# Gate logits and the branch merge of a hybrid attention/recurrence layer with tokens as rows

## The chip, the core and the metric

One Trainium2 chip, one of its NeuronCores. The number is the device time of one execution in microseconds, the median of several runs.

## What is computed

One layer of a backbone over 256 latent tokens with a prefix of 256 context tokens, width 2048, everything in 32-bit floating point. The mixer part matters here, cut to its core:

```python
p = h @ w_in                       # h: normed, modulated tokens
c_q, c_kv, k_r, hg_q, hg_ff, hg_fb, hg_i, hg_g, gate_logits = split(p)
attn_o = attention(...)            # 8 heads of 128, latent and context keys
hg_o = rmsnorm(hgrn2(...)) * silu(hg_g)          # 8 heads of 128
y_a = attn_o.reshape(256, 1024) @ w_br_mla       # (256, 2048)
y_h = hg_o.reshape(256, 1024) @ w_br_hgrn        # (256, 2048)
g = sigmoid(gate_logits)                         # (256, 2, 2048)
out = (g[:, 0] * y_a + g[:, 1] * y_h) @ w_out
x = x + gt_a * rmsnorm(out)        # then a SwiGLU part, 2048 -> 2 x 5632 -> 2048
```

## The kernel before, in words

A matmul takes a stationary operand (128 x up to 128) and a moving one (128 x up to 512). Each 32-bit operand is split into a high part H, rounded to the format that TensorE multiplies quickly, and a low rest L; a product is then three: high by high, high by low, low by high. Activations are split once. Weights come in tiles of 1 MB (`load_w`, L100, on SP's queue, three buffers `raw`), and each tile is split in two halves of 1024 columns: ACT casts H (L108), DVE subtracts to get L (L110). There are three buffers of each, so ACT casts a half when TensorE has read the half that was in the buffer.

Two layouts of a product occur. With channels as rows the weight is stationary (128 x 128) and the tokens move: `mm3` (L144) and, for the latent tokens alone, `mm_wide`, where one product has H against both token parts (512 columns, L148) and one L against the high part (256 columns, L149). With tokens as rows 128 tokens are stationary and 512 weight columns move: `project_tok` (L825), which serves the output projection and the SwiGLU part, with two accumulators `pst`, one for each half of the tokens.

PSUM has eight banks of 128 x 512. Four belong to the pool `pj` (the long accumulators), which rotates through them, four to `px` (short ones).

The stages in order: adaLN vectors and the first projections; eight recurrent heads (`hgrn_head`); attention in four pairs of heads. Since attention is made of short steps, 32 blocks of the gate logits (`gates`, each 16 pairs of L148 and L149) are put between them. A pair of heads begins with `att_q`: queries `pq` and rope queries `pr` from one weight tile (L654, L144), then values `pv2` from another (L670), then a gate block; then come keys (`att_k`), scores with softmax (`att_s`, whose rope half uses 64 of 128 rows, L698), transposes (`att_t`) and values (`att_v`). Gate logits go to DRAM (`sgd`) by POOL's queue, since no room is left for them, and come back in the merge. The merge runs over 16 blocks of 128 channels: both branches as 48 products of 256 columns in one bank (`psb`, L760), sigmoid on ACT, product on DVE (L763), sum of the branches on POOL (L765), split into `units`. Jobs that multiply a tile of adaLN weights on DVE (`mod_job`) are strewn over all stages. After the output projection comes the SwiGLU part; its product rows are turned by TensorE transposes (`turn`, L961).

The order on each engine is not the one in the text: a scheduler places instructions by estimated times of its own, and each engine then works strictly in its order.

## Time and profile before

| | us |
|---|---|
| median of three runs | 1741.63 (1738.98, 1741.84, 1741.63) |
| the profiled execution, time | 1740.55 |
| the profiled execution, span from first to last instruction | 1738.8 |
| gates and attention, from the first gate product to the first merge product | 533.1 to 808.4 |
| merge, to the first product of the output projection | 808.4 to 900.7 |
| TensorE (PE) busy | 1694.0 |
| VectorE (DVE), ScalarE (ACT), GpSimd (POOL) busy | 1089.0, 766.2, 51.7 |
| mean granted clock of TensorE | 0.991 |

PE's weight loads (PEld) are listed apart from its products. A product's duration in the profile runs from its start to a modelled end, and the next one starts before that; the distance between starts tells what a product costs. "Idle before <- releaser" names what ended a wait.

### The profile page before, as it was taken

How to read it: one execution, taken by the hardware profiler on the slowest of the kernel's cores; microseconds unless marked ns; L12 is line 12 of the kernel's file. 1: busy time of each engine (PE TensorE's matmuls, PEld its weight loads, DVE VectorE, ACT ScalarE, POOL GpSimd, SP SyncE). 2: the span in 40 equal slices, each digit the busy share in tenths (PEclk: the TensorE clock that was granted, in tenths of full speed). 3: DMA queues.
4: the chain of work that ended last, by engine and by line, in shares of the span. 5: the costliest groups of instructions: out<-in, count | busy, mean ns of one | idle time of the engine just before them, and what ended most of it. 6: DMA issues, size and time to landing. Idle time of an engine off the chain costs nothing.

```text
span 1738.8 us, 22134 instructions
## 1 busy us (share of the span) xinstructions
PE 1694.0 (97%) x8715; PEld 1410.4 (81%) x8715; DVE 1089.0 (63%) x1619; ACT 766.2 (44%) x1086; POOL 51.7 (3%) x81
## 2 busy tenths in 40 slices
PE   6898999999999999999999899999999999999997
PEld 4457888888888888889998788888888888888886
DVE  5335777777778766666765765664456655544456
ACT  5225443343345444445544554444444443344443
POOL 0100000000000000001210000000000000000000
PEclk9899999999999999999999999999999999999999
DMA  9983455655556565578766456665566665555653
GB/s 389 357 330 148 162 178 194 217 194 194 180 183 231 193 253 189 194 290 303 278 222 224 167 218 242 234 234 187 194 242 233 234 233 208 194 193 185 214 193 121
DMA packets 60247, 383.78 MB, mean 221 GB/s; under 512 B 7104, under 2 KB 7920, under 8 KB 16880
## 3 DMA queue, kind: packets, MB, share of 16 engines
q1 hardware_dynamic: 55328, 368.15, 58.1%
q0 software_dynamic: 4096, 13.11, 1.9%
q8 instruction: 68, 1.11, 0.3%
q10 hardware_dynamic: 720, 1.12, 0.2%
q14 instruction: 35, 0.29, 0.0%
HBM read 376.03 MB, written 6.32 MB: 220 GB/s over the span
## 4 chain that ended last, share of the span: by engine, by line
PE 94%; DMA 2%; DVE 2%; ACT 1%; issue 0%; SPq 0%; DVEq 0%; ACTq 0%
PE pst L825 45%; PE ps L144 13%; PE ps L148 11%; PE ps L149 5%; PE psb L760 5%; PE pre L144 3%; DMA raw<-in_wm_dram 2%; PE pm L282 1%; PE pst L919 1%; PE psS L698 1%; PE po L722 1%; PE psS L695 1%; PE pv L670 1%; PE pq L654 1%; PE pk L144 1%; PE pgt L961 1%
## 5 line engine op out<-in xcount | busy, mean ns | idle before, releaser
L110 DVE TENSOR_TENSOR wL<-raw,wH 128x1024 fp32r<-128x1024 f32 x480 | 589.8, 1231 | 480.0 <-ACT wH L108 458.2
L108 ACT CAST wH<-raw 128x1024 fp32r<-128x1024 f32 x480 | 503.4, 1050 | 710.8 <-PE pst L825 393.1
L825 PE MATMUL pst<-wH,hx 128*128 128x512 f32 x2272 | 660.6, 390 | 0.0
L825 PEld LDWEIGHTS pst<-wH,hx 128*128 128x128 f32 x2272 | 425.6, 188 | 87.7
L825 PE MATMUL pst<-wL,hx 128*128 128x512 f32 x1136 | 402.2, 389 | 0.0
L148 PE MATMUL ps<-hx,wH 128*128 128x512 f32 x832 | 300.6, 402 | 2.8 <-DVE lat L367 2.8
L825 PEld LDWEIGHTS pst<-wL,hx 128*128 128x128 f32 x1136 | 213.2, 188 | 44.4
L149 PE MATMUL ps<-hx,wL 128*128 128x256 f32 x832 | 235.6, 284 | 0.0
L144 PE MATMUL ps<-hx,wH 128*128 128x512 f32 x672 | 212.5, 395 | 0.0
L148 PEld LDWEIGHTS ps<-hx,wH 128*128 128x128 f32 x832 | 156.9, 189 | 40.2 <-DVE lat L367 3.1
L346 DVE CUSTOM_DVE_ANT_0 raw<-raw,cb 128x2048 f32<-128x2048 f32 x64 | 146.1, 2283 | 31.8 <-DMA raw<-in_wm_dram 31.6
L149 PEld LDWEIGHTS ps<-hx,wL 128*128 128x128 f32 x832 | 157.7, 190 | 3.3 <-DVE mx L700 1.1
L144 PEld LDWEIGHTS ps<-hx,wH 128*128 128x128 f32 x672 | 125.0, 188 | 25.2
L144 PE MATMUL ps<-hx,wL 128*128 128x512 f32 x336 | 131.7, 392 | 0.0
L144 PEld LDWEIGHTS ps<-hx,wL 128*128 128x128 f32 x336 | 63.1, 188 | 12.8
L144 PE MATMUL pre<-hx,wH 128*128 128x512 f32 (+1 forms) x204 | 66.7, 410 | 5.4 <-ACT hx L201 5.3
L144 PEld LDWEIGHTS pre<-hx,wH 128*128 128x128 f32 x204 | 39.6, 204 | 25.6 <-ACT hx L201 10.8
L760 PE MATMUL psb<-hx,wH 128*128 128x256 f32 x256 | 46.8, 283 | 0.0
L760 PE MATMUL psb<-hC,wH 128*128 128x256 f32 x256 | 46.8, 283 | 0.0
L760 PEld LDWEIGHTS psb<-hx,wH 128*128 128x128 f32 x256 | 39.9, 192 | 0.0
L760 PEld LDWEIGHTS psb<-hC,wH 128*128 128x128 f32 x256 | 39.9, 192 | 0.0
L282 PE MATMUL pm<-raw,cst 128*32 128x512 f32 (+1 forms) x320 | 34.9, 538 | 4.3 <-DMA raw<-in_wm_dram 4.2
(256 smaller groups left out, 1416.8 us busy)
## 6 DMA issues: line engine op xcount, KB each, us to landing
raw<-in_wm_dram SPq DMA_DIRECT2D x96, 1024.0 KB, 4.9
raw<-in_wfi_dram SPq DMA_DIRECT2D x88, 1024.0 KB, 4.8
raw<-in_win_dram SPq DMA_DIRECT2D x73, 1024.0 KB, 4.8
raw<-in_wfo_dram SPq DMA_DIRECT2D x44, 1024.0 KB, 4.8
raw<-in_wbr_dram SPq DMA_DIRECT2D x16, 1024.0 KB, 5.6
raw<-in_wout_dram SPq DMA_DIRECT2D x16, 1024.0 KB, 4.9
raw<-in_wqk_dram SPq DMA_DIRECT2D x4, 1024.0 KB, 5.3
sgd<-sgx POOLq DMA_DIRECT2D x16, 256.0 KB, 5.0
```

What stands on the lines that cost most here:

```text
L108: nc.scalar.copy(H, raw[:, o:o + n])
L110: nc.vector.tensor_tensor(L, raw[:, o:o + n], H.bitcast(F32), op=ALU.subtract)
L144: nc.tensor.matmul(o, l, r, start=(first and i == 0), stop=(last and i == len(seq) - 1))
L148: nc.tensor.matmul(ps, w[0], act.rearrange("p e t -> p (e t)"), start=first, stop=False)
L149: nc.tensor.matmul(ps[:, 0:T], w[1], act[:, 0, :], start=False, stop=last)
L282: nc.tensor.matmul(pm[32 * (k % 4):32 * (k % 4) + 32, 0:n], cst[:, k], raw[:, kk * n:(kk + 1) * n], start=(k < 4), stop=(k >= KD - 4))
L346: nc.vector.tensor_tensor_reduce(out=raw, in0=raw, in1=cbt[0], scale=1.0, scalar=0.0, op0=ALU.mult, op1=ALU.add, accum_out=mod2[:, i // KD ...
L654: nc.tensor.matmul(pq[:, i * T:(i + 1) * T], l, r, start=(k == 0 and i == 0 and z == 0), stop=(k == 3 and i == 1 and z == 2))
L670: nc.tensor.matmul(pv[:, i, :], ckvs[:, k, l, ts_], r, start=(i == 0 and k == 0 and z == 0), stop=(i == 1 and k == 1 and z == 2))
L695: nc.tensor.matmul(psS, qn[a][:, i * T + qb * P:i * T + (qb + 1) * P], kn[b], start=(n == 0), stop=False)
L760: nc.tensor.matmul(ps[:, br * T:(br + 1) * T], l, r, start=(br == 0 and k == 0 and z == 0), stop=(br == 1 and k == NH - 1 and z == 2))
L825: mm = nc.tensor.matmul(ps[hf], l, r, start=(k == 0 and n == 0), stop=(k == nk - 1 and n == 2))
```

## The change

The gate logits and both branches of the merge go from channels as rows to tokens as rows. `gates` now works on chunks of 512 of the 4096 gate columns: four calls share two accumulators `psg`, one for each token half, and each call takes one 1 MB tile with 4 of the 16 k blocks, 24 products of 512 columns. After the fourth call the two rows are copied out (one by ACT, one by DVE) and stored. The merge has four chunks of 512 channels; each branch of a chunk goes through `project_tok`; the gates are multiplied onto the accumulators, POOL adds the branches, and the rows are turned back into `units` by eight transposes a chunk (`turn_merged`), called after the first tile of the next chunk. The long banks are no longer one pool of four but two pairs, `pj` and `pk`: other users alternate, the gate accumulators take `pk`, the attention tiles `pj`. The adaLN jobs in the merge keep their number, five.

```diff
+    def bank(name, tag=None, shape=(P, 512)):
+        if tag is None:
+            tag = ("pj", "pk")[n_bank[0] % 2]
+            n_bank[0] += 1
+        return pj.tile(list(shape), F32, tag=tag, name=name)
...
     def gates(b):
-        j = b // 2
+        cc, q = b // 4, b % 4
         if b % 2 == 0:
             mod_job(1)
-        w = split_w(load_w(win[47 + b - NPRE]))
-        ps = pj.tile([P, 512], F32, tag="pj", name="ps")
-        for k in range(KD):
-            mm_wide(ps, w(k * P, P), hx[:, 0, k], k == 0, k == KD - 1)
-        half = sgx[:, j % 4, (b % 2) * T:(b % 2 + 1) * T]
-        nc.scalar.copy(half, ps[:, 0:T])
-        nc.vector.tensor_tensor(half, half, ps[:, T:2 * T], op=ALU.add)
-        if b % 2 == 1:
-            nc.gpsimd.dma_start(sgd[j], sgx[:, j % 4, :])
+        w = split_w(load_w(wg[cc, q]))
+        if q == 0:
+            gate_ps[:] = [bank("psg", "pk") for _ in range(2)]
+        for k in range(4 * q, 4 * q + 4):
+            H, L = w(k % 4 * 512, 512)
+            for hf in range(2):
+                aH, aL = (hx[:, 0, k, e, hf * P:(hf + 1) * P] for e in range(2))
+                for n, (l, r) in enumerate(((aH, H), (aL, H), (aH, L))):
+                    nc.tensor.matmul(gate_ps[hf], l, r, start=(k == 0 and n == 0), stop=(k == KD - 1 and n == 2))
+        if q == 3:
+            for hf in range(2):
+                row = sgx[:, (2 * cc + hf) % 4, :]
+                (nc.scalar.copy if hf else nc.vector.tensor_copy)(row, gate_ps[hf])
+                nc.gpsimd.dma_start(sgd[cc, hf], row)
         step()
...
     def att_q(p, A):
-        pq = pj.tile([P, 512], F32, tag="pj", name="pq")
-        pr = pj.tile([P, 512], F32, tag="pj", name="pr")
+        pq = bank("pq", "pj")
+        pr = bank("pr", "pj")
...
-            pv = pj.tile([P, 2, T], F32, tag="pj", name="pv2")
+            pv = bank("pv2", "pj", (P, 2, T))
...
-    for j in range(KD):
-        sg = sgx[:, (4 + j) % 8, :]
-        nc.gpsimd.dma_start(sg, sgd[j])
-        w = split_w(load_w(wbr[j]))
-        ps = pj.tile([P, 512], F32, tag="pj", name="psb")
-        for br, src in enumerate(([aT[:, h] for h in range(NH)], hgT)):
-            for k in range(NH):
-                H, L = w(br * 1024 + k * P, P)
-                for z, (l, r) in enumerate(((H, src[k][:, 0, :]), (H, src[k][:, 1, :]), (L, src[k][:, 0, :]))):
-                    nc.tensor.matmul(ps[:, br * T:(br + 1) * T], l, r, start=(br == 0 and k == 0 and z == 0),
-                                     stop=(br == 1 and k == NH - 1 and z == 2))
-        nc.scalar.activation(sg, sg, AF.Sigmoid)
-        nc.vector.tensor_tensor(sg, ps, sg, op=ALU.mult)
-        m = wk.tile([P, T], F32, tag="hf", name="m", bufs=2)
-        nc.gpsimd.tensor_tensor(m, sg[:, 0:T], sg[:, T:2 * T], op=ALU.add)
-        dst = units[j]
-        split_act(dst, m)
-        mg.append(dst)
-        if j % 3 == 0 and j < 13:
-            mod_job(1)
...
+    def turn_merged(c):
+        for b in range(0, 4, 2):
+            pt = px.tile([P, 2, T], F32, tag="px", name="pmt")
+            for i in range(2):
+                for hf in range(2):
+                    nc.tensor.matmul(pt[:, i, hf * P:(hf + 1) * P], m_row[c][hf][:, (b + i) * P:(b + i + 1) * P], ident,
+                                     is_transpose=True, start=(i + hf == 0), stop=(i + hf == 2))
+            for i in range(2):
+                dst = units[4 * c + b + i]
+                split_act(dst, pt[:, i])
+                mg.append(dst)
+
+    m_row = []
+    for c in range(4):
+        sg = []
+        for n in range(4):
+            sg.append(sgx[:, 4 * (c + 1) % 8 + n, :])
+            nc.gpsimd.dma_start(sg[n], sgd[2 * c + n // 2, n % 2])
+        for br, src in enumerate(([aT[:, h] for h in range(NH)], hgT)):
+            ps = project_tok(lambda q: wbr[br, c, q], NH, lambda k: src[k], True, True, None,
+                             (lambda: turn_merged(c - 1)) if c > 0 and br == 0 else None)
+            for hf in range(2):
+                g = sg[2 * br + hf]
+                nc.scalar.activation(g, g, AF.Sigmoid)
+                nc.vector.tensor_tensor(g, ps[hf], g, op=ALU.mult)
+                if br == 1:
+                    nc.gpsimd.tensor_tensor(sg[hf], sg[hf], g, op=ALU.add)
+        m_row.append(sg)
+        mod_job(2 if c == 0 else 1)
...
         ps = project_tok(lambda q: wout[c, q], KD, lambda k: mg[k], True, True,
-                         pairs([wide(u) for u in spare[:8]]) if c == 3 else None)
+                         pairs([wide(u) for u in spare[:8]]) if c == 3 else None,
+                         (lambda: turn_merged(3)) if c == 0 else None)
```

The weights are laid out anew to suit (`wg`, `wbr` as tiles of 4 k blocks by 512 columns). The scheduler makes another order of it. Three places follow; the numbers of the lines are those of the kernel that the order belongs to, and a number in a name tells two tiles of one name apart.

PE at the end of `att_q` of the second pair of heads, before: queries, rope queries, and the values right behind.

```order
L654 MATMUL pq<-cqkv,wH 128x256 x2
L654 MATMUL pq<-cqkv,wL 128x256
L144 MATMUL pr<-cqkv,wH 128x256 x2
L144 MATMUL pr<-cqkv,wL 128x256
L670 MATMUL pv_5200<-wH,cqkv 128x256 x2
L670 MATMUL pv_5200<-wL,cqkv 128x256
```

The same place in the changed kernel.

```order
L671 MATMUL pq<-cqkv,wH 128x256 x2
L671 MATMUL pq<-cqkv,wL 128x256
L154 MATMUL pr<-cqkv,wH 128x256 x2
L154 MATMUL pr<-cqkv,wL 128x256
L634 MATMUL psg<-wH,hx 128x512 x4
L687 MATMUL pv_5099<-wH,cqkv 128x256 x2
L687 MATMUL pv_5099<-wL,cqkv 128x256
```

Four products of the next gate tile's first half now stand between pr and the first of the two value tiles; the second value tile comes after eight more gate products. The other three pairs of heads have four gate products in the same place.

ACT at the last head, before: the exponentials (L704) of the last head's two score tiles, and only then the sigmoids of the merge (L762).

```order
L108 CAST wH<-raw 128x1024 x2
L619 COPY sgx<-ps 128x256
L704 ACTIVATE sgx,mx<-psS,mx 128x512 x2
L108 CAST wH<-raw 128x1024
L762 ACT_TABLE_LOAD
L762 ACTIVATE sgx<-sgx 128x512 x3
L619 COPY sgx<-ps 128x256
L725 COPY of<-po_6705 128x256
```

The same place in the changed kernel, where L721 is the exponential and L823 the sigmoid.

```order
L118 CAST wH<-raw 128x1024
L638 COPY sgx<-psg 128x512
L823 ACT_TABLE_LOAD
L823 ACTIVATE sgx<-sgx 128x512
L742 COPY of<-po_6416 128x256
L142 CAST hx<-of 128x256
L721 ACT_TABLE_LOAD
L721 ACTIVATE sgx,mx<-psS,mx 128x512
L823 ACT_TABLE_LOAD
L823 ACTIVATE sgx<-sgx 128x512
L721 ACT_TABLE_LOAD
L721 ACTIVATE sgx,mx<-psS,mx 128x512
```

Sigmoids and exponentials alternate now, with a table load at each turn; two weight casts follow.

PE in the merge, at the start of the second chunk in the changed kernel, where `pmt` is the turned tile of the first chunk.

```order
L794 MATMUL pst<-wH,hx 128x512 x4
L805 MATMUL pmt<-c_82,sgx 128x128 x2
L794 MATMUL pst<-wL,hx 128x512
L794 MATMUL pst<-wH,hx 128x512 x2
L794 MATMUL pst<-wL,hx 128x512
L805 MATMUL pmt<-c_82,sgx 128x128 x6
```

The transposes stand 28 to 32 products behind the end of the chunk whose rows they turn. Up to the first gate product, but for two products that are swapped, and from the transposes ahead of the SwiGLU part on, the order on PE is the old one.

More of the change, by code (lines that the diff above doesn't have):

```diff
@@ L680, in att_k @@
     def att_k(i, A):
-        pk = pj.tile([P, 512], F32, tag="pj", name="pk2")
+        pk = bank("pk2", "pj")
         for k in range(2):
@@ L789, in rows @@
-    def rows(i, vec, tiles):
-        pg = px.tile([P, 512], F32, tag="px", name="pg")
-        nc.tensor.transpose(pg[0:KD, 0:P], vec, ident)
-        grow = wk.tile([KD, P], F32, tag="scs", name="grow")
-        nc.scalar.copy(grow, pg[0:KD, 0:P])
-        nc.sync.dma_start(gdr[i], grow)
-        for c, g in enumerate(tiles):
-            nc.sync.dma_start(g, gdr[i, 4 * c:4 * c + 4].rearrange("k p -> (k p)").partition_broadcast(P))
-        return tiles
     def project_tok(tiles, nk, src, first, last, lead=None, hook=None):
-        ps = [pj.tile([P, 512], F32, tag="pj", name="pst") for _ in range(2)]
+        ps = [bank("pst") for _ in range(2)]
@@ L830, in sqrt_table, with rows @@
+    def rows(i, vec, tiles):
+        pg = px.tile([P, 512], F32, tag="px", name="pg")
+        nc.tensor.transpose(pg[0:KD, 0:P], vec, ident)
+        grow = wk.tile([KD, P], F32, tag="scs", name="grow")
+        nc.scalar.copy(grow, pg[0:KD, 0:P])
+        nc.sync.dma_start(gdr[i], grow)
+        for c, g in enumerate(tiles):
+            nc.sync.dma_start(g, gdr[i, 4 * c:4 * c + 4].rearrange("k p -> (k p)").partition_broadcast(P))
+        return tiles
     def sqrt_table(dep):
@@ L903, in first_chunk @@
     def first_chunk():
-        ps = [pj.tile([P, 512], F32, tag="pj", name="pst") for _ in range(2)]
+        ps = [bank("pst") for _ in range(2)]
         raws = [load_w(wfi[0, 1]), load_w(wfi[0, 2])]
```

44 lines of the change are left out of this document (22 added, 22 removed).

## The prediction, made before the changed kernel was run

> **What bounds it now.** I read the page's first part, then the stretches that the edit touches.
>
> ```profile
> PE 1694.0 (97%) x8715; PEld 1410.4 (81%) x8715; DVE 1089.0 (63%) x1619; ACT 766.2 (44%) x1086; POOL 51.7 (3%) x81
> ```
>
> ```profile
> 533.10:808.30 275.20, 275.20 (x1589) 234.78 (x1588) 190.49 (x311) 134.16 (x234) 11.91 (x22) 1.00 0.63 231
> 808.30:900.70 92.40, 92.40 (x772) 92.37 (x771) 69.31 (x74) 45.76 (x60) 19.96 (x25) 1.00 0.71 261
> 900.70:982.00 81.30, 81.30 (x361) 67.28 (x360) 44.46 (x44) 39.29 (x52) 0.73 (x1) 1.00 0.66 237
> ```
>
> The columns are length, then busy time of PE, weight load, DVE, ACT and POOL, the granted clock, the DMA share and GB/s. The first row holds the gates and attention, the second the merge, the third most of the output projection. PE is busy all the time in each, at full clock. So the time changes by what the edit does to PE's own work, plus any hole it opens. What DVE, ACT or POOL gain is worth nothing by itself.
>
> A matmul's listed duration is no price, since matmuls overlap. The price is the distance between starts, read from the chain that ended last (start, length, count):
>
> ```profile
> 825.98 74.62 PE psb L760 x622
> 900.72 81.64 PE pst L825 x360
> 1049.36 0.87 PE pgt L961 x8
> 1094.64 43.54 PE pst L825 x192
> ```
>
> A merge product 256 wide costs (900.72 - 825.98) / 622 = 120.2 ns. A token-row product 512 wide costs 81.64 / 360 = 43.54 / 192 = 226.8 ns, less than two of the other (240.4 ns). A 128 x 128 transpose costs 0.87 / 8 = 109 ns. The old gate form is a pair, one 512 wide and one 256 wide; the timeline shows its distance in two runs:
>
> ```profile
> 674.79 0.40 PE L148 MATMUL ps<-hx,wH 128*128 128x512 f32 x1
> ...
> 676.91 0.40 PE L148 MATMUL ps<-hx,wH 128*128 128x512 f32 x1
> ...
> 708.14 0.40 PE L148 MATMUL ps<-hx,wH 128*128 128x512 f32 x1
> ...
> 714.04 0.39 PE L148 MATMUL ps<-hx,wH 128*128 128x512 f32 x1
> ```
>
> Six pairs in 2.12 us are 353 ns each, seventeen in 5.90 us are 347 ns.
>
> **Part by part.** *Gate logits.* There are 32 blocks of 16 pairs, 512 in all; now 8 chunks of 16 k, two token halves and three products, 768 of 512 columns. Before 512 x 0.350 = 179.2 us, after 768 x 0.2268 = 174.2 us: **-5.0** (-3.5 at 347 ns, -6.5 at 353). The column count is the same; what goes is the fixed part of a third kind of product.
>
> *Merge.* Before 768 x 0.1202 = 92.3 us. After 384 x 0.2268 = 87.1 us and 32 transposes x 0.109 = 3.5 us: **-1.7**. Eight of the transposes fall in the first projection chunk, which changes the place, not the sum.
>
> *Score products.* The order interleaves gate products more finely with the attention scores. The half of a score that uses 64 rows pays at its border:
>
> ```profile
> 697.08 0.40 PE L695 MATMUL psS<-spH,spL 128*128 128x512 f32 x1
> 697.40 0.49 PE L698 MATMUL psS<-spH 64*128 64x512 f32 x1
> ...
> 697.97 0.39 PE L698 MATMUL psS<-spH,spL 64*128 64x512 f32 x1
> 698.29 0.50 PE L695 MATMUL psS<-spL,spH 128*128 128x512 f32 x1
> ```
>
> ```profile
> PEld psS L698 <- issue: 6.0, 17, 0.4
> ```
>
> Going in takes 0.32 us for 0.23, going out too: 0.2 us a group. The old order has 17 such groups (the waits view counts 17), the new one 21: **+0.8** (0 to 1).
>
> *The long banks in two pairs.* The four attention tiles pq, pr and twice pv2 now share two banks, where they rotated through four. Before, the value products of pv2 stand right behind pr and find free banks. After, they must wait until pr is copied out, and the next gate products are put ahead of them. Those need a fresh half of split weights, whose buffer is the one that the last pq product reads:
>
> ```profile
> 683.02 1.06 ACT L108 CAST wH<-raw 128x1024 fp32r<-128x1024 f32 x1 [3.01 <-PE pq L654]
> 683.98 0.58 ACT L636 CAST spH<-pq 128x512 fp32r<-128x512 f32 x1
> 684.45 0.38 ACT L658 COPY qr<-pr 128x256 f32<-128x256 f32 x1
> ```
>
> ```profile
> 683.18 0.28 PE L144 MATMUL pr<-cqkv,wL 128*128 128x256 f32 x1
> 683.30 0.40 PE L670 MATMUL pv<-wH,cqkv 128*128 128x256 f32 x2
> ```
>
> Today the cast hides under 24 value products (2.9 us). In the new order PE is free at 683.30 and the cast ends at 684.08: a hole of 0.78 us, 0.83 with the hand-over that I allow. The pr copy ends at 684.83, 1.53 us behind the free point, while four gate products behind the hole reach 0.83 + 0.9 = 1.7, so the bank itself costs nothing more. The cast stands alike for the other pairs of heads:
>
> ```profile
> 621.13 1.05 ACT L108 CAST wH<-raw 128x1024 fp32r<-128x1024 f32 x1 [3.01 <-PE pq L654]
> 744.79 1.05 ACT L108 CAST wH<-raw 128x1024 fp32r<-128x1024 f32 x1 [3.01 <-PE pq L654]
> 557.43 1.05 ACT L108 CAST wH<-raw 128x1024 fp32r<-128x1024 f32 x1 [3.95 <-issue]
> ```
>
> Four holes: **+3.3** (0 if other work fills them, 6 if the bank is late too). Behind the hole nothing else is late: ACT and DVE do their work from the same releases.
>
> *Gate banks.* A chunk owns both pk banks, so the next one waits for two copies of 128 x 512 out of PSUM:
>
> ```profile
> L763 DVE TENSOR_TENSOR sgx<-psb,sgx 128x512 f32<-128x512 f32 x16 | 11.0, 691 | 5.7 <-PE psb L760 5.7
> ```
>
> The shortest cover in the new order is four transposes and the other half's three last products, 0.44 + 0.68 = 1.1 us, against 0.3 us until a product has ended and 0.69 for the copy: 1.0. I take **+0** for the seven hand-overs and keep 0.5 each, 3.5, as the upper end.
>
> *Evacuation.* The 32 copies and 32 additions of the old gate blocks go, 16 copies come; all of it lies beside PE. The merged rows pass mult (0.69), a POOL addition and the transposes. POOL takes 1.75 us for 128 x 512:
>
> ```profile
> L1017 POOL TENSOR_TENSOR y<-y,x x2: 1736/1748/1760, 1726.1 to 1731.6; 128x512 f32<-128x512 f32 x2
> ```
>
> The second half's addition is done about 3 us after the chunk's last product, and its transposes stand 32 products, 7.3 us, behind it. Weight bytes and loads are the same in number; the four xr loads move ahead of four gate weights on SP, behind the same wait for the last key product, with some 20 us of loaded gate work as cover. None costs anything.
>
> *ACT at the last head.* The sigmoids of the merge now stand between the last exponentials: four more table loads. The parts, from rows of today:
>
> ```profile
> 784.46 1.05 ACT L108 CAST wH<-raw 128x1024 fp32r<-128x1024 f32 x1 [0.73 <-PE ps L148]
> 785.53 1.28 ACT L762 ACT_TABLE_LOAD   x1
> 786.82 1.67 ACT L762 ACTIVATE sgx<-sgx 128x512 f32<-128x512 f32 x3
> ...
> 789.07 0.37 ACT L725 COPY of<-po 128x256 f32<-128x256 f32 x1 [0.32 <-PE po L722]
> ```
>
> ```profile
> L704 ACT ACTIVATE sgx<-psS,mx 128x512 f32<-128x512 f32 x16 | 10.9, 688 | 23.2 <-DVE mx L701 23.2
> L110 DVE TENSOR_TENSOR wL<-raw,wH 128x1024 fp32r<-128x1024 f32 x480 | 589.8, 1231 | 480.0 <-ACT wH L108 458.2
> ```
>
> Count from the last product of the seventh gate chunk. PE has 8 score products, 8 passes of the value product and 36 gate products to do, 2.3 + 1.7 + 8.2, then 0.3 of transposes: the next weight half is wanted at 12.5 us, its low part at 13.4. ACT does cast, gate copy, four table loads, two sigmoids, the head's copy and cast (not before 4.2) and two exponentials, then that half's cast at 12.1; DVE follows at 13.3. It fits by some 0.3 us: **+0.3** (0 to 2).
>
> Sum: -5.0 - 1.7 + 0.8 + 3.3 + 0.3 = -2.3. The profiled execution took 1740.55 us (1.75 outside its span); that makes 1738.3, I say **1738.5 us**. The runs shown are 1738.98, 1741.84 and 1741.63, median 1741.63, so the profiled execution is an ordinary one. A measurement of this kernel can tell about 0.2%, 3.5 us, from no change; the forecast lies inside it.
>
> Two rules speak against the change. The Trainium skill, TensorE: Matmul & The Clock Gate, "Wait — 56ns, not 53.3ns?", gives a warm product N / 2.4 GHz plus 2.5 ns, whatever N; that would be 109 and 216 ns, estimated from that page, where the rows have 120 and 227, so the trace does not agree for these operands. The Trainium skill, ScalarE: Activation LUTs, "What ACT_TABLE_LOAD costs", adds a drain of 1.38 us to each switch, which would put 5.5 us more on ACT at the last head and open a hole of about 5 us; the rows above show cast, load and sigmoid end to end with no drain.
>
> **Rivals.** *No hole at pq* (0.20): the four casts are covered after all. For it: today's stretch has not one hole. Against: the order puts nothing else there. Time 1738.3 - 3.3 = 1735.0, faster.
>
> *Gate banks late* (0.17): the copies stand in the strict order of DVE and ACT behind casts of 1.05 and subtractions of 1.23 us. Seven times 0.5 gives 1742, within the band.
>
> *Sigmoids block the casts* (0.10), the slower one. A sigmoid waits in ACT's order for a gate row to come back from DRAM, and the weight cast behind it feeds PE.
>
> ```profile
> DMA to landing us min/median/max: 2.3/4.4/8.0
> ```
>
> ```profile
> 811.22 0.55 POOL L622 DMA_DIRECT2D sgd<-sgx  x1 [9.44 <-DVE sgx L620]
> 814.68 0.54 POOL L753 DMA_DIRECT2D sgx<-sgd  x1 [2.91 <-DMA sgd<-sgx]
> ...
> 819.12 0.63 ACT L762 ACTIVATE sgx<-sgx 128x512 f32<-128x512 f32 x1 [1.16 <-DMA sgx<-sgd]
> ```
>
> At the merge's start the load of the second chunk's row waits for the last gate row's write. With 3.5 and 4.4 us, as here, it lands 9.6 us into the merge, the cast behind it ends at 11.3, and its low part at 12.6, wanted at 14.5. If write and load take 8.0 each, that is 20.7: a hole of 6.2, and 1.6 more at the last head in the same way: 1738.5 + 7.8 = 1746.3. It decides from about 10 us for both; the trace has 7.9.
>
> *The fixed part is not saved* (0.05): the new products cost 240 ns, two of today's 256-wide ones, because a weight load stands ahead of each. For it: in the merge the weight loads are busy 92.37 of 92.40 us. Gates then cost 768 x 0.240 = 184.6 (+5.4), the merge 92.3 + 3.5 (+3.5): 1740.55 + 8.9 + 4.4 = 1753.9. Against it: the projection's 360 products have the same operand forms and take 226.8. By the rule of the Trainium skill's TensorE page above the gates would change by -0.6 and the merge by +2.5 (an estimate from that page), 1747 us with the other terms; its chance lies within these 0.05.
>
> **Numbers.** The forecast has 0.48. Faster takes the first rival and 0.12 of the forecast's low side (pairs at 353 ns): 0.32. Slower takes the last two: 0.15. The rest, 0.53, is no change that can be told. The range runs from 1734 (no holes, pairs dear) to 1744 (bank hand-overs and late landings in part).
>
> **What would show it.** Right: gate and merge products at 227 ns; four holes of 0.8 us with PE waiting for ACT's wH behind pr; the transposes at 109 ns with no wait on POOL. Wrong: holes at the first products of a gate chunk, ACT idle on sgx with PE idle soon after, or products above 227 ns.

## The result and the profile after

The changed kernel takes **1750.64 us** (median of four runs, 1748.43 to 1753.53), the kernel before 1741.43 beside it: a ratio of 1.0054, 95% interval 1.0042 to 1.0066. It is 9 us slower. A second series, which stands below as an experiment, gave 1749.95 against 1741.77, 1.0051 (1.0039 to 1.0063). The forecast was 1738.5 with a range up to 1744.

The busy time by engine, from the first part of the page, and the three stretches that the edit touches (gates and attention, merge, output projection), with the columns as in the prediction:

```profile
PE 1697.8 (97%) x8107; PEld 1381.6 (79%) x8107; DVE 1080.6 (62%) x1595; ACT 765.0 (44%) x1066; POOL 50.4 (3%) x73
```

```profile
536.24:814.96 278.72, 275.06 (x1332) 221.72 (x1331) 183.32 (x286) 135.12 (x214) 10.93 (x20) 1.00 0.61 223
814.96:908.84 93.88, 91.44 (x411) 74.06 (x410) 66.13 (x72) 43.52 (x58) 16.93 (x18) 1.00 0.74 272
908.84:999.42 90.58, 88.16 (x393) 72.67 (x392) 51.87 (x62) 45.20 (x69) 3.53 (x2) 1.00 0.60 218
```

The same stretches of the kernel before:

```profile
533.10:808.21 275.11, 275.11 (x1589) 234.69 (x1587) 190.49 (x311) 134.15 (x233) 11.91 (x22) 1.00 0.63 232
808.21:900.47 92.26, 92.26 (x772) 92.23 (x771) 69.25 (x73) 45.60 (x59) 19.96 (x25) 1.00 0.71 260
900.47:990.21 89.74, 87.31 (x388) 71.98 (x385) 49.91 (x58) 44.51 (x67) 0.73 (x1) 1.00 0.61 220
```

PE's busy time hardly moved in any of them (275.06 for 275.11, 91.44 for 92.26, 88.16 for 87.31). Before, the first two had no idle time at all. Now 278.72 - 275.06 = 3.7 us and 93.88 - 91.44 = 2.4 us are idle. Stretch by stretch the change costs 3.6, 1.6 and 0.8 us, 6.1 in all. Another 3.1 us stand ahead of it, since the first gate product begins at 536.24 instead of 533.10. What PE waits for in these stretches, from the view of waits (engine, line, what it waited for: us in total, times, longest):

```profile
PE psg L634 <- ACT wH L118: 2.6, 4, 0.7
PE psg L634 <- ACT sgx L638: 1.0, 1, 1.0
PE pst L794 <- DVE wL L120: 2.4, 2, 1.5
PEld psS L715 <- issue: 7.6, 21, 0.4
```

Four waits for ACT's cast were forecast. One bank hand-over (`sgx` copied out of `psg`) is late by 1.0 us. Two waits for low weight parts stand in the merge, where the forecast had none. The last row counts the score groups with 64 rows: 21, as the order had it.

**The first hole of the merge**, engine by engine. POOL stores the two rows of the last gate chunk and fetches rows for the second merge chunk into the same buffers; ACT's sigmoid waits for the first of them with two casts behind; DVE makes the low parts; PE waits:

```profile
815.47 0.54 POOL L639 DMA_DIRECT2D sgd<-sgx  x1 [12.18 <-DVE sgx L638]
816.76 0.55 POOL L639 DMA_DIRECT2D sgd<-sgx  x1 [0.75 <-ACT sgx L638]
821.25 1.16 POOL L817 DMA_DIRECT2D sgx<-sgd  x2 [3.94 <-DMA sgd<-sgx]
...
827.01 0.63 ACT L823 ACTIVATE sgx<-sgx 128x512 f32<-128x512 f32 x1 [5.58 <-DMA sgx<-sgd]
827.55 1.98 ACT L118 CAST wH<-raw 128x1024 fp32r<-128x1024 f32 x2
...
828.62 1.23 DVE L120 TENSOR_TENSOR wL<-raw,wH 128x1024 fp32r<-128x1024 f32 x1 [5.93 <-ACT wH L118]
829.76 0.68 DVE L824 TENSOR_TENSOR sgx<-pst,sgx 128x512 f32<-128x512 f32 x1
830.36 2.28 DVE L356 CUSTOM_DVE_ANT_0 raw<-raw,cb 128x2048 f32<-128x2048 f32 x1
832.57 0.08 DVE L356 DVE_READ_ACCUMULATOR2_ANT mod<- 128x1 f32 x1
832.57 0.69 DVE L824 TENSOR_TENSOR sgx<-pst,sgx 128x512 f32<-128x512 f32 x1
833.17 2.35 DVE L120 TENSOR_TENSOR wL<-raw,wH 128x1024 fp32r<-128x1024 f32 x2
...
834.44 0.50 PE L794 MATMUL pst<-wL,hC 128*128 128x512 f32 x1 [1.54 <-DVE wL L120]
```

Which store the fetch waits for can be read from the transfers of `sgd` in this window, two stores and two fetches, from issue to landing:

```profile
DMA to landing us min/median/max: 4.8/5.5/5.7
```

None landed sooner than 4.8 us behind its issue, so the store of 816.76 was under way until after 821.5, when the first fetch had been issued already (821.25). That fetch waited for the store ahead, of 815.47. The row is there 11.5 us after this store was issued (815.47 to 827.01), 12.0 us into the merge. The two casts end at 829.53, but the second low part starts only at 833.17: in DVE's order two gate multiplications and an adaLN job of 2.28 us stand ahead of it. PE wanted it at 832.74 and has it at 834.44. So two things come together, a late row in ACT's order and a job in DVE's, and the experiments have to say which of them is needed.

### The profile page after: what moved, and what is told of

The parts are those of the page before. It is cut to its first block, busy times and chain, and to the rows that moved or that the text cites. A ratio compares the mean times of both kernels' runs of the same rounds, so it can differ in the third digit from the quotient of the medians.

```text
span 1748.0 us, 20859 instructions
## 1 busy us (share of the span) xinstructions
PE 1697.8 (97%) x8107; PEld 1381.6 (79%) x8107; DVE 1080.6 (62%) x1595; ACT 765.0 (44%) x1066; POOL 50.4 (3%) x73
## 3 DMA queue, kind: packets, MB, share of 16 engines
q0 software_dynamic: 4096, 13.11, 2.0%
## 4 chain that ended last, share of the span: by engine, by line
PE 90%; DMA 3%; DVE 2%; issue 2%; ACT 1%; POOL 0%; SPq 0%; DVEq 0%; ACTq 0%; POOLq 0%
PE pst L794 48%; PE ps L154 13%; PE psg L634 9%; PE pre L154 4%; PE ps L158 4%; PE ps L159 2%; DMA raw<-in_wm_dram 2%; PE pm L292 1%; PE pst L947 1%; PE psS L715 1%; PE psS L712 1%; PE po L739 1%; PE pv L687 1%; PE pq L671 1%; PE pk L154 1%
## 5 line engine op out<-in xcount | busy, mean ns | idle before, releaser
L794 PE MATMUL pst<-wH,hx 128*128 128x512 f32 x2400 | 699.0, 390 | 0.0
L794 PEld LDWEIGHTS pst<-wH,hx 128*128 128x128 f32 x2400 | 449.5, 188 | 92.7
L154 PE MATMUL ps<-hx,wH 128*128 128x512 f32 x672 | 212.4, 395 | 0.0
L634 PE MATMUL psg<-wH,hx 128*128 128x512 f32 x512 | 158.2, 398 | 3.7 <-ACT wH L118 2.6
L154 PEld LDWEIGHTS ps<-hx,wH 128*128 128x128 f32 x672 | 125.0, 188 | 25.3
L158 PE MATMUL ps<-hx,wH 128*128 128x512 f32 x320 | 116.7, 405 | 2.8 <-DVE lat L377 2.8
L634 PEld LDWEIGHTS psg<-wH,hx 128*128 128x128 f32 x512 | 94.4, 188 | 26.6 <-ACT wH L118 3.8
L634 PE MATMUL psg<-wL,hx 128*128 128x512 f32 x256 | 97.0, 397 | 0.0
L159 PE MATMUL ps<-hx,wL 128*128 128x256 f32 x320 | 91.8, 287 | 0.0
L158 PEld LDWEIGHTS ps<-hx,wH 128*128 128x128 f32 x320 | 60.8, 190 | 17.2 <-DVE lat L377 3.1
L154 PEld LDWEIGHTS ps<-hx,wL 128*128 128x128 f32 x336 | 63.1, 188 | 12.8
L159 PEld LDWEIGHTS ps<-hx,wL 128*128 128x128 f32 x320 | 61.2, 191 | 0.9 <-issue 0.2
L634 PEld LDWEIGHTS psg<-wL,hx 128*128 128x128 f32 x256 | 47.3, 188 | 11.7 <-issue 1.7
```

The lines of the kernel that those rows point to most:

```text
L154: nc.tensor.matmul(o, l, r, start=(first and i == 0), stop=(last and i == len(seq) - 1))
L158: nc.tensor.matmul(ps, w[0], act.rearrange("p e t -> p (e t)"), start=first, stop=False)
L159: nc.tensor.matmul(ps[:, 0:T], w[1], act[:, 0, :], start=False, stop=last)
L634: nc.tensor.matmul(gate_ps[hf], l, r, start=(k == 0 and n == 0), stop=(k == KD - 1 and n == 2))
L794: mm = nc.tensor.matmul(ps[hf], l, r, start=(k == 0 and n == 0), stop=(k == nk - 1 and n == 2))
```

## The experiments

Times alone do not separate these causes well. In every kernel below, what lies between a product at about 187 us (the 901st PE record) and the end is steady but for the edited stretches, while the first 187 us wander by several us from run to run. So each kernel is read by its stretches first; "gates", "merge" and "projection" are the three from above.

| kernel | gates | merge | projection | first part, profile | time, median | ratio to before |
|---|---|---|---|---|---|---|
| before | 275.1 | 92.3 | 89.7 | 185.9 | 1741.4 | |
| changed | 278.7 | 93.9 | 90.6 | 189.0 | 1750.6 | 1.0054 (1.0042 to 1.0066) |
| changed, again | 278.8 | 95.3 | 90.6 | 186.6 | 1750.0 | 1.0051 (1.0039 to 1.0063) |
| bank pairs only | 282.9 | 92.3 | 89.7 | 188.8 | 1749.0 | 1.0039 (1.0024 to 1.0055) |
| new gates, old merge | 281.9 | 93.9 | 89.7 | 190.7 | 1749.9 | 1.0044 (1.0029 to 1.0059) |
| old gates, new merge | 283.3 | 90.4 | 90.6 | 189.0 | 1748.9 | 1.0044 (1.0030 to 1.0057) |
| pr elsewhere | 273.5 | 96.9 | 90.6 | 188.7 | 1746.3 | 1.0025 (1.0017 to 1.0033) |
| last rows at hand | 279.1 | 91.0 | 90.6 | 186.0 | 1743.9 (one run) | |
| adaLN jobs moved | 279.7 | 90.7 | 90.6 | 189.3 | 1749.6 (one run) | |
| full rows | 272.6 | 94.4 | 90.6 | 187.7 | 1742.8 (one run) | |
| before, full rows | 268.7 | 92.3 | 89.7 | 186.1 | 1734.9 | 0.9962 (0.9949 to 0.9974) |
| rows kept | 279.4 | 90.9 | 90.6 | 186.0 | 1744.7 | 1.0022 (1.0013 to 1.0030) |
| all mended | 266.1 | 93.3 | 90.7 | 191.0 | 1735.8 | 0.9962 (0.9948 to 0.9976) |
| mended, jobs back | 266.1 | 90.1 | 90.6 | 191.8 | 1731.1 | 0.9932 (0.9916 to 0.9947) |

### The pairs of banks alone

```diff
-        pq = pj.tile([P, 512], F32, tag="pj", name="pq")
-        pr = pj.tile([P, 512], F32, tag="pj", name="pr")
+        pq = bank("pq", "pj")
+        pr = bank("pr", "pj")
...
-            pv = pj.tile([P, 2, T], F32, tag="pj", name="pv2")
+            pv = bank("pv2", "pj", (P, 2, T))
...
-        ps = pj.tile([P, 512], F32, tag="pj", name="ps")
+        ps = bank("ps", "pk")
```

> The kernel before, with nothing changed but the long banks: two pairs, the four attention tiles pq, pr and pv2 and the key tiles on one pair, the gate blocks on the other, all else alternating. Theory (the pair of banks makes the four holes): the order now puts one gate product ahead of the value products behind pr, in each of the four pairs of heads, so PE waits there 0.8 us for ACT's cast, four times, 3.3 us; 16 score groups with 64 rows instead of 17 give back 0.4: about 1744.3 us against 1741.4, and PE waits for wH right behind pr in the trace. Rival (holes come from the gate products' new form, not from the banks): 1741.0, no such wait. Second question, the start: in the changed kernel's profiled execution the first gate product began 3.1 us later than before (536.2 for 533.1), in two stretches of lower granted clock. If the bank pairs do that, this kernel's first gate product stands at 536 too and the time is 1747; if it is chance, it is near 533 here or wanders between runs.

Measured 1749.03 us, and the gate stretch is 7.8 us longer, where the theory had 2.9, and more than in the changed kernel itself. The waits of PE:

```profile
PE ps L157 <- ACT wH L117: 2.0, 3, 0.7
PE ps L158 <- DVE wL L119: 1.8, 2, 1.0
PE pv L679 <- ACT qr L667: 0.8, 3, 0.3
```

The hole behind pr appears, 0.82 us by the distance of starts, in three of the four pairs of heads. Here the bank is late as well: the value product behind the one gate product waits for the copy of pr (`qr`), another 0.53 us each. Two waits for a low part, 0.93 and 1.20, stand at the gate blocks in between. Together 6.2 of the 7.8 us; the rest is not at one place. So the holes come from the pairs of banks, not from the new form of the gate products, and the old gate blocks suffer more from the pairs than the new ones: on top of the pairs the new form gains 282.9 - 278.7 = 4.2 us. The new form with one pool of four banks was not run. On the second question, the start: the first gate product stands at 536.0 here, but between 533.2 and 539.1 in the kernels below with the same pairs, so this one place decides nothing.

### The gates without the merge, and the merge without the gates

The changed kernel with the old merge loop:

```diff
-    for c in range(4):
-        sg = []
...
-            ps = project_tok(lambda q: wbr[br, c, q], NH, lambda k: src[k], True, True, None,
...
+    for j in range(KD):
+        sg = sgx[:, (4 + j) % 8, :]
+        nc.gpsimd.dma_start(sg, sgd[j // 2, j % 2])
...
+        ps = bank("psb")
```

The changed kernel with the old gate blocks:

```diff
-        w = split_w(load_w(wg[cc, q]))
-        if q == 0:
-            gate_ps[:] = [bank("psg", "pk") for _ in range(2)]
...
+        w = split_w(load_w(win[47 + b - NPRE]))
+        ps = bank("ps", "pk")
+        for k in range(KD):
+            mm_wide(ps, w(k * P, P), hx[:, 0, k], k == 0, k == KD - 1)
...
+            nc.gpsimd.dma_start(sgd[j // 2, j % 2], sgx[:, j % 4, :])
```

> The changed kernel with the old merge (channels as rows, 16 blocks, products of 256 columns). Left out: the gate rows are stored in the new layout and read in the old one, so each gate value lands on another token and channel; the work is the same. Theory: the stretch from the first gate product to the first merge product keeps its loss (278.7 us for 275.1 before: holes 3.3, a late bank 1.2, four more score borders of 0.41 us, against 3.4 gained by the gate products), the merge is 92.4 again: 1745 us, and 1748 if the start's 3.1 us belong to the change. Rival (the gates gain as forecast, the loss is the merge's): 1740.

> The kernel before with the bank pairs and the new merge, but the old gate blocks (channels as rows, pairs of products). Left out: the gate values are read in another layout than stored, so they land on other tokens and channels; the work is the same. Theory: the merge with its transposes costs 2.4 us more than the old one (two holes of 1.7 and 1.0 us in which PE waits for the low weight parts, the rest of the gain eaten at borders), the bank pairs 2.9: 1746.7 us. Rival (the two holes come from the late gate rows alone, which the old gate blocks store two at a time and earlier): the merge gains 0.3 and the time is 1744.

Neither sum came out (1749.88 and 1748.86 us), and both for reasons that say something. The first keeps the changed kernel's holes in the gate stretch; on top come a wait of 1.1 us for a low part and, at its end, one of `psb` for the last gate copy, since both now use the same pair. And the *old* merge, which had no wait before, has two for low parts here, and takes 93.9 us instead of 92.3:

```profile
PE psb L808 <- DVE sgx L638: 1.2, 1, 1.2
PE psb L808 <- DVE wL L120: 1.2, 2, 0.8
```

This points to the rows of the new gate blocks rather than to the new merge: here too ACT's sigmoid waits for a fetched row, 5.07 us long, until 12.0 us into the merge. In the second kernel, with the old gate blocks, the sigmoid at that place in ACT's order starts 10.5 us into the merge, 1.5 us earlier, and PE waits nowhere in the new merge:

```profile
819.63:910.06 90.43, 90.41 (x413) 74.36 (x412) 65.78 (x72) 43.42 (x58) 15.83 (x16) 1.00 0.75 274
910.06:1000.64 90.58, 88.15 (x394) 72.68 (x392) 51.87 (x62) 45.18 (x69) 3.54 (x2) 1.00 0.61 220
```

Against 92.26 and 89.74 it gains 1.83 and gives back 0.84 for the eight transposes in the projection: -1.0 us. This is the price of the merge's new form in this kernel. By the distance of starts one low part still comes 0.3 us late in it, and in the last kernel below the same sum is -1.3 us. The gate stretch of this kernel loses what the pairs alone lose (283.3 for 282.9).

### pr in a short bank

```diff
-        pr = bank("pr", "pj")
+        pr = px.tile([P, 512], F32, tag="px", name="pr")
```

> The changed kernel, with pr in one of the four short banks instead of the pair pj, so that the first pv2 finds a free bank. The order then has 12 value products (1.44 us) behind pr, more than the 0.78 us for which PE waited on the cast, and 19 score groups with 64 rows instead of 21. Theory: the holes at pr go (at three of four pairs of heads at least; the first pair's order differs), 2.5 to 3.3 us, and 0.8 from the borders: 1746.5 to 1747.5 us against 1750.6. Rival (the cast is late whatever stands there, the hole moves to the next gate product): 1749.8, and PE waits for wH as long as before, a dozen products later.

Measured 1746.26 us. All four holes at pr are gone, the gate stretch falls from 278.7 to 273.5 us and is now 1.6 shorter than before: the theory holds, and the hole did not move to the next gate product. (The 5.2 us are 1 more than the theory's 3.3 and 0.8; where the rest comes from is open.) But the merge of the profiled execution grew by 3 us. Its second hole, first DVE's rows, then PE's:

```profile
848.15 2.29 DVE L356 CUSTOM_DVE_ANT_0 raw<-raw,cb 128x2048 f32<-128x2048 f32 x1 [1.25 <-DMA raw<-in_wm_dram]
850.37 0.08 DVE L356 DVE_READ_ACCUMULATOR2_ANT mod<- 128x1 f32 x1
850.37 1.22 DVE L120 TENSOR_TENSOR wL<-raw,wH 128x1024 fp32r<-128x1024 f32 x1
...
851.64 0.89 PE L794 MATMUL pst<-wL,hC 128*128 128x512 f32 x2 [2.23 <-DVE wL L120]
```

The adaLN job stands in DVE's order ahead of the low part and here waits 1.25 us for its own weights. The low part, whose cast had ended at 846.79 (started 845.74, 1.05 long), waits with it. How long this job waits differs between executions of one program: not at all in the first profile of the changed kernel, 1.92 us in the second.

### Late rows or adaLN jobs

Two kernels: first the last rows at hand, then the adaLN jobs moved to the recurrent heads.

```diff
-                nc.gpsimd.dma_start(sgd[cc, hf], row)
+                if cc < 7:
+                    nc.gpsimd.dma_start(sgd[cc, hf], row)
...
-            nc.gpsimd.dma_start(sg[n], sgd[2 * c + n // 2, n % 2])
+            if c == 1 and n >= 2:
+                continue
+            nc.gpsimd.dma_start(sg[n], sgd[min(2 * c + n // 2, 6), n % 2])
```

```diff
-            mod_job(4 if h < NH - 1 else 3)
+            mod_job(5 if h < 5 else 4)
...
-        mod_job(2 if c == 0 else 1)
```

> The changed kernel; the last gate chunk's two rows are neither stored nor fetched: the second merge chunk's second branch takes the two rows that lie in the buffers (they are the last chunk's, so it has other gates), and the last merge chunk fetches an earlier chunk's rows. The order of every engine's work is otherwise the same. Theory A (the first hole of the merge, 1.7 us, needs the late row: ACT's sigmoid waits 5.6 us for it and the cast behind it feeds PE): that hole is gone; the second, 1.0 us, which stands at other rows, stays: merge 92.2 us instead of 93.9. Theory B (the holes come from the adaLN jobs that stand in DVE's order ahead of the low weight parts, whatever the rows do): both stay, 93.9. If both need the late rows: 91.2.

> The changed kernel with the merge's five adaLN jobs done in the recurrent heads instead (five jobs a head for the first four, four for the last). Theory B (an adaLN job of 2.3 us in DVE's order ahead of a low weight part makes each hole): both holes of the merge are gone, merge 90.5 to 91.2 us instead of 93.9, although ACT still waits for the late row. Theory A (late rows alone): the first hole stays at 1.7, 93 us. The recurrent stage (347.27 us in every run so far) may lose up to 2 us if DVE has no room there. 20 score groups with 64 rows instead of 21: 0.4 us less in the gate stage.

With the rows at hand the first hole is gone: merge 90.97, beyond what theory A gave. The second is 0.7 us instead of 1.0, a difference within what the job's own wait makes of it from one execution to the next. Without the jobs both holes are gone as well, merge 90.69, although ACT waits for the row as long as before:

```profile
830.06 0.63 ACT L823 ACTIVATE sgx<-sgx 128x512 f32<-128x512 f32 x1 [5.59 <-DMA sgx<-sgd]
```

So neither theory is right alone. The late row takes the slack, the job takes what is left; either one taken away closes the first hole. The jobs have to go somewhere, though: the recurrent stage, 347.27 us before, takes 349.03 with the five, and the gate stretch 1 us more than in the changed kernel, so that little of the gain is left.

### Scores on 128 rows

```diff
+    qzH = wk.tile([P, 2, T], F32R, tag="kt", name="qzH")
+    qzL = [wk.tile([P, T], F32R, tag="hf", name="qzL", bufs=2) for _ in range(2)]
...
-                nc.tensor.matmul(psS, qr[a][rr, qsl], krs[b][rr, :], ...)
+                nc.tensor.matmul(psS, qr[a][:, qsl], krs[b], ...)
```

The rope queries of each head now lie in a tile of 128 rows, in which the rows of the other head are zeros.

> The changed kernel with the rope half of the scores on 128 rows: each head's rope queries are put beside 64 rows of zeros, so that the key tile, which holds the rope keys twice, is taken whole. Same products, same columns, same results. Theory (a score group with 64 rows costs 0.41 us at its two borders, 17 groups 6.95 us before, 21 groups 8.76 us in the changed kernel): the gate and attention stage takes 278.7 - 8.7 = 270.0 us. Rival (the extra time is that of waiting for the softmax and its buffers, which the groups only show): 277 to 279.

> The kernel before with the rope half of the scores on 128 rows in the same way. Theory: 17 groups at 0.41 us: the gate and attention stage takes 275.1 - 6.9 = 268.2 us and the time 1734.4 us against 1741.3. Rival (ACT's and DVE's four additional small operations in each pair of heads delay the casts by as much): 1740 to 1742.

The kernel before takes 1734.91 us in this form against 1742.45 beside it; its gate stretch is still without idle time and 6.4 us shorter:

```profile
533.34:802.04 268.70, 268.70 (x1588) 237.22 (x1587) 191.71 (x315) 135.15 (x237) 12.79 (x25) 1.00 0.65 237
```

That is 0.38 us for each of 17 groups, with the same number of products and columns, and the 17 waits of weight loads at these groups (`issue`, 6.0 us before) are gone from the view of waits. The count from the trace of before (what the distances of starts have above 226.8 ns, from the product ahead of a group to the second one behind it) was 6.95 us, 0.41 each. In the changed kernel 6.2 of 8.7 us are gained; the waits at pr and new ones behind the scores take part of it back (five waits for wH, 3.3 us in all, instead of four with 2.6).

### Rows kept

```diff
+    gate_at = (0, 1, 4, 5, 6, 7, 2, 3)
...
-        w = split_w(load_w(wg[cc, q]))
+        w = split_w(load_w(wg[gate_at[cc], q]))
...
-                nc.gpsimd.dma_start(sgd[cc, hf], row)
+                if cc < 6:
+                    nc.gpsimd.dma_start(sgd[gate_at[cc], hf], row)
...
-            nc.gpsimd.dma_start(sg[n], sgd[2 * c + n // 2, n % 2])
+            if c != 1:
+                nc.gpsimd.dma_start(sg[n], sgd[2 * c + n // 2, n % 2])
```

> The changed kernel with the gate chunks computed in another order, so that the last two computed are the ones that the second merge chunk needs, and lie in the buffers where it looks for them: four rows are neither stored nor fetched; the result is the reference's. Theory (the merge loses 2.9 us to gate rows that land late in front of a cast, and the adaLN jobs do the rest): merge 91.0 us as with the rows at hand, all else as in the changed kernel: its own part from the recurrent heads on 2.9 us shorter. Rival (the rows of the third chunk now come late in their place): 93.9.

Here nothing is left out of the result. Merge 90.93 us, and the view of waits has none of PE in it (by the distance of starts two low parts are still 0.4 and 0.3 us late); 1744.71 us in all: theory right.

```profile
812.58:903.51 90.93, 90.78 (x412) 74.31 (x410) 65.94 (x72) 43.74 (x58) 14.75 (x14) 1.00 0.74 268
```

### The changed kernel once more

> The changed kernel once more, unchanged. Its first 189 us (to a product amid the first projections) took 188.97 us in the profile, 185.87 before, with equal instructions on TensorE but for two that are swapped; from there to the end every run was steady. Chance: the start wanders between 185.5 and 191 us in all kernels, so that more runs of the changed kernel lie about 1747 to 1749 us, nearer than the 1750.6 of the first four, 6 to 7 us above the kernel before. Rival (the change makes the start slower): 1750.6 again, 9 us above.

1749.95 us, near the first series, but not for the reason of the rival. The first part took 186.59 us in this profile and 188.97 in the first, with the same program; so the 3.1 us of the first profile need not come from the change. What was longer this time is the merge, 95.30 us, by the second hole, in which the adaLN job waits for its weights:

```profile
851.32 2.29 DVE L356 CUSTOM_DVE_ANT_0 raw<-raw,cb 128x2048 f32<-128x2048 f32 x1 [1.92 <-DMA raw<-in_wm_dram]
```

From the 901st record on the changed kernel is 6.2 us behind in the first profile and 7.6 in this one (1748.01 - 188.97 - 1738.75 + 185.87, and 1747.1 - 186.59 - 1738.75 + 185.87). The rest of the 8 to 9 us between the medians is not located: the first part wanders, and so does the second hole. Against a longer start speaks the kernel with the rows kept, whose first part is the same work: its median of 11 runs less what its profile has outside the first part is 186.9 us, and the same for the kernel before beside it 187.1 (estimates that take the later part as steady).

### All of it together

Two kernels: both have pr in a short bank, the rows kept and the full rows; the first has this edit as well, the second has not.

```diff
-        mod_job(2 if c == 0 else 1)
+        mod_job((2, 0, 2, 1)[c])
```

> The changed kernel with all that the runs point to: rows of the last two computed gate chunks kept, pr in a short bank, rope scores on 128 rows, and the adaLN job behind the second merge chunk moved behind the third. Sum from the runs: gates and attention 273.5 (pr elsewhere) less 6.2 (full rows) = 267.3 us, merge 90.4, output projection 90.6: together 448.3 against 451.1 for the kernel before with full rows (268.7, 92.3, 89.7 in the profile), and against 457.1 for the kernel before. Expected 1732 to 1733 us, 9 us under the kernel before and 2 to 3 under the kernel before with full rows. Rival (pr elsewhere and full rows make new places where a cast is late, as the full rows alone did in the changed kernel with about 1.5 us): 1734 to 1736, no better than the kernel before with full rows.

> The kernel with everything mended, but the adaLN jobs of the merge where the changed kernel has them (two behind its first chunk, one behind each other). In the run before it the merge took 93.34 us: holes of 1.5 and 0.7 us where two jobs stood behind the third chunk, while the rows kept alone gave 90.9. Theory (the moved job made those holes): merge 90.9 us, gates and attention 266.1, so 1731.5 us with a usual start of 187 us, 10 us under the kernel before and 3 under the kernel before with full rows (1734.9). Rival (pr elsewhere or the full rows make the holes): merge 92.5 to 93.5 and 1733.5 to 1734.

The first took 1735.80 us: gates 266.1, 1.2 less than summed, but two jobs behind one chunk make new holes, a wait of 1.4 us for wH and one of 0.6 for wL. With the jobs back the merge has no wait at all, and the kernel takes **1731.06 us**, a ratio of 0.9932 (0.9916 to 0.9947) to the kernel before, which took 1743.42 beside it:

```profile
539.09:805.21 266.12, 265.12 (x1333) 224.69 (x1331) 184.76 (x290) 134.33 (x216) 9.61 (x19) 1.00 0.63 229
805.21:895.29 90.08, 90.08 (x411) 74.47 (x410) 65.99 (x72) 44.00 (x58) 14.76 (x14) 1.00 0.75 271
895.29:985.87 90.58, 88.16 (x393) 72.70 (x392) 51.82 (x62) 45.20 (x69) 3.53 (x2) 1.00 0.61 218
```

The three stretches take 446.8 us, against 450.7 for the kernel before with full rows and 457.1 for the kernel before. So the new layout is worth 3.9 us beyond the full rows with these mends. One hole is still open, the late gate bank with 1.0 us.

## Why the prediction was wrong

By the terms of its sum, for the first profiled execution (borders and products from the distances of starts):

| term | forecast | measured |
|---|---|---|
| gate products, where they follow one another | -5.0 | -4.7 |
| score groups with 64 rows | +0.8 | +1.8 |
| holes at pr | +3.3 | +3.3 |
| gate banks | 0 (to 3.5) | +1.2 |
| other borders among the gate products | 0 | +2.0, by difference |
| merge, its form | -1.7 | -1.0 |
| merge, holes | 0 | +3.4 (+4.9 the second time) |
| last head's ACT | +0.3 | 0 |
| the first 189 us | 0 | +3.1 (+0.7 the second time) |

**The holes at pr** were right in place, cause and size. PE, then ACT, at the third pair of heads:

```profile
687.03 0.28 PE L154 MATMUL pr<-cqkv,wL 128*128 128x256 f32 x1
687.97 1.20 PE L634 MATMUL psg<-wH,hx 128*128 128x512 f32 x4 [0.66 <-ACT wH L118]
...
686.88 1.05 ACT L118 CAST wH<-raw 128x1024 fp32r<-128x1024 f32 x1 [2.79 <-PE pq L671]
```

The next start is 0.94 us behind the last pr product instead of 0.12, four times. The rival without them (chance 0.20) is out, and the run with pr elsewhere shows the cause. Even "so the bank itself costs nothing more" held here, with four gate products to cover it; with the one product that the bank pairs alone put there, it cost 0.53 us.

**The step that failed** is the weighing of the rival "Sigmoids block the casts". Its mechanism is what happened. It said that the row lands 9.6 us into the merge, that the cast behind it ends at 11.3 and its low part at 12.6, and that it decides from about 10 us for write and load together, for which the trace had 7.9. Measured are 12.0, 13.6 and 14.9 us, and 11.5 for both. The step counted from the last row's store, 1.7 us into the merge; the load waits for the store ahead of it, 0.5 us into the merge. So write and load were taken 3.6 us too short, and the row came 2.4 us later than forecast, where 2.1 us were to spare. The 7.9 us stood at one place of the kernel before. Another place, 30 us earlier in the same trace, has one row stored and one fetched (POOL's rows, then the times from issue to landing of `sgd` there):

```profile
781.00 0.55 POOL L622 DMA_DIRECT2D sgd<-sgx  x1 [4.88 <-DVE sgx L620]
787.61 0.54 POOL L753 DMA_DIRECT2D sgx<-sgd  x1 [6.07 <-DVE mx L705]
...
DMA to landing us min/median/max: 6.2/6.3/6.3
```

From the first issue to the second landing that is 12.8 us, beyond the 10 at which the rival decides. What makes these transfers slow at one place and not at another is not shown.

The step also followed one half of the weights only. The first half's low part came when it was wanted (14.5 forecast, a loss of 0.2 us). The second half's stands behind two multiplications and an adaLN job in DVE's order, 3.4 us more, and this queue was not counted. A place with 2 us of slack and an uncounted queue was given 0.10. Of the 11.5 us between the sum and the profiled execution (1738.3 and 1749.8) this step makes 3.4, more than any other; 3.1 are the first part, and the rest is spread over the other rows of the table.

**The merge's form** gains 1.0 us in the kernel with the old gate blocks and 1.3 in the last one, not 1.7. Products and transposes have the forecast price: a run of transposes costs only some 0.01 us more at its borders. Two more transposes in the merge (`pg`, of the adaLN vectors) were not in the sum, 0.2 us; in the first of these kernels a low part is 0.3 us late besides, and the rest is spread.

**Gate products and borders.** Where pair follows pair, the one of before cost 351.5 ns in the mean, for 350 taken, and the new product 228.3 instead of 226.8 (distances over 0.3 us, which stand at borders, left out). That makes 180.0 and 175.3 us, near the forecast. The 2.0 us at other borders are what the stretch's +3.6 leaves after the other rows; they were not traced one by one. A score group costs 0.41 us and not 0.2: four distances are stretched by some 0.1 us each (into the group, behind its first product, out of it, and behind the next product), and the prediction read off two. Four groups more make 1.8 us. The gate copies were late once in seven hand-overs, by more than the 0.5 us allowed for each, and behind a subtraction on DVE and a cast on ACT, as that rival had it.

**The price per product** was no danger: products with the weight loaded ahead do not cost 240 ns, and the rule of the Trainium skill that gives 2.5 ns above N / 2.4 GHz (TensorE: Matmul & The Clock Gate, "Wait — 56ns, not 53.3ns?") does not fit here either: 228.3 and 226.8 ns for 512 columns are 15.0 and 13.5 above N / 2.4 GHz. PE waits nowhere for POOL's sum, as said.

The range ended at 1744 since each small unknown was placed low. What the sum took as zero came out above it: banks +1.2, other borders +2.0, late rows with the jobs behind them +3.4.

## What to carry to other kernels

Where an instruction that waits for a DMA is put into the order of an engine that also prepares operands, count to the end of the queue behind it, on that engine and on the next, for every operand and not for the first alone, and take the longest round trip that the trace shows, not the one at the same place (7.9 us at the same place, 12.8 us 30 us earlier, and 11.5 came). Splitting one pool of banks in two takes freedom from all its users: price it by itself, since here it cost more (7.8 us) than the layouts gained (4.2 and 1.0). A gain of layout may be real and still invisible until the holes that it opens are closed one by one.

## What the runs showed of the hardware

**A change between 128 and 64 rows costs.** Some 0.4 us at each group of products with 64 rows, as weight loads wait at the group ("issue", 21 times, 0.4 us the longest). Zeros in the other 64 rows remove it. The Trainium skill, TensorE: Matmul & The Clock Gate, "Step-by-step: what each phase is for", says that a weight load's time does not depend on the row count, and that loads are pulled ahead of running products when the row groups do not conflict or the load goes to the background weight buffer. The loss stands exactly at the borders between 128 and 64 rows in this trace, which fits a conflict of row groups but does not show one; no run here times a load by its rows alone.

**The clock may fall after a hole, or not.** Behind the hole of 2.6 us in the kernel with pr elsewhere, the granted clock was 0.50 for 3.1 us, and seven products in a row cost 427 ns each instead of 227, 1.4 us lost beside the hole. Behind 3.1 us in the second profile of the changed kernel it stayed at 1.00:

```profile
849.00:851.60 2.60, 0.41 (x2) 0.00 (x0) 2.60 (x4) 2.60 (x4) 0.00 (x0) 1.00 0.09 13
852.30:855.40 3.10, 3.10 (x9) 2.40 (x8) 2.16 (x2) 0.00 (x0) 0.00 (x0) 0.50 0.99 394
```

```profile
851.70:854.80 3.10, 0.37 (x2) 0.00 (x0) 3.10 (x4) 3.01 (x4) 0.00 (x0) 1.00 0.10 26
854.80:858.00 3.20, 3.19 (x14) 2.61 (x15) 2.83 (x3) 0.02 (x1) 0.00 (x0) 1.00 0.86 340
```

The first part of the program wanders in the same way. In the first profile of the changed kernel two stretches near 97 and 141 us ran at 0.59 and 0.62, in that of before at 1.00:

```profile
96.00:98.00 2.00, 2.00 (x9) 1.58 (x6) 0.26 (x1) 0.00 (x0) 0.00 (x0) 0.59 1.04 436
139.00:143.00 4.00, 4.00 (x13) 3.17 (x12) 0.72 (x2) 0.00 (x0) 1.90 (x2) 0.62 0.87 369
```

In the second profile of the changed kernel, the same program, these two stretches ran at 1.00 and 0.86. A comparison of two single profiles would have put these 3 us on the change.
